# The last embedding's gate tiles 4 to 7 as seven Strassen block products, in a two-layer decoder step

## The chip, the cores and the metric

The kernel runs on one core of one Trainium2 chip. The metric is the device time of one execution in microseconds (us). In the profile the core's engines are PE (matrix multiply; PEld is its weight load), DVE (vector), ACT (scalar, with the activation functions), POOL (GpSimd) and SP (which issues the DMAs). Every computing engine takes its instructions in the order in which they stand in its queue.

## The reference

The kernel computes one inference step of a two-layer decoder for 512 prompt tokens and 32 sample tokens, in float32. Each layer ends with a gated embedding, and the change touches the second layer's, the last work of the kernel:

```python
D_MODEL, PLE_DIM = 1024, 256
def rmsnorm(x, g):
    xf = x.astype(jnp.float32)
    y = xf * lax.rsqrt(jnp.mean(xf * xf, axis=-1, keepdims=True) + EPS)
    return (y * g.astype(jnp.float32)).astype(x.dtype)
...
            h = h + 0.5 * swiglu(rmsnorm(h, ffn2_norm[i]), ffn2_w1[i], ffn2_w3[i], ffn2_w2[i])
            gate = jax.nn.sigmoid(rmsnorm(h, ple_norm[i]) @ ple_w_gate[i])
            h = h + gate * (pe[i] @ ple_w_proj[i])
```

## The kernel before, in words

The residual stream `h` lies transposed in SBUF, as eight chunks of 128 features by 544 tokens (T = 544, half of it HT = 272). Every float32 product is made of three float32r matmuls: weight and input are each split into a rounded part `hi` and a rest `lo`, and hi·hi, hi·lo and lo·hi are added in PSUM (`mm`, L286, L290, L292). A weight tile's split is an ACT cast and a DVE subtraction of 128x1024 (`_split`, L242 and L243); an input's is the same on 128x544 (`split_pair`, L330 and L331). One matmul takes 272 columns, so that an output tile of 128 features takes 8 x 3 x 2 = 48 matmuls.

The feed-forward layers already use a Strassen form with seven products in place of eight (`seven`, `forms`, `products`). Four weight blocks of 128x1024 give seven weight pieces, for four of which DVE makes a sum first (`_sum`, L228). The input side needs sums too: `forms` takes two chunks of `h`, scales both on ACT (L352), makes two combined tiles on DVE (one subtraction of 544 columns, L356, and two of 272, L358 and L359), and splits each into hi and lo (L330 on ACT, L331 on DVE). One product is 24 matmuls.

The last feed-forward layer ends with eight output tiles of its second matrix. After each, `update` adds it to the chunk `h[c]` on DVE (L578), and `on_chunk` (in `next_norm`) prepares the next norm: ACT scales by the gain (L342), DVE makes the rest (L343), ACT squares (L369) and POOL adds the square to `acc` (L371). The order on PE, DVE, ACT and POOL inside the feed-forward layer is the order of the code (`manual_schedule`); in the embedding the framework's scheduler orders each queue.

`ple` then makes the gates: eight tiles of 48 matmuls over the eight chunks in order. Beside the first or second of them `rstd` sums the squares over the partitions with four small matmuls (L408) and ACT and DVE make the reciprocal root (L386 to L393). Until that is done the gate tiles stay in PSUM; then DVE multiplies a tile by `rstd` (L766) and ACT takes the sigmoid (L767). A product with the embedding's own input follows two tiles behind (12 matmuls), is multiplied into the gate (L777), added to `h` (L778) and stored. There are three PSUM accumulators of the large kind (`ps`), used in turn, and two small ones (`pb`). Tile 7 is made in two column halves (`ple_last`), so that only a half's gate, product, sum and store follow the last matmul.

Weights are taken in the order of the list `pieces`; `prepare` loads, sums and splits them a few places ahead (`ahead`, 2 or 3 for splits and sums). Where the changed kernel is spoken of, its line numbers stand beside its own names: `ssq` and `update` have moved to L408, L410 and L617, the gate's multiplication and sigmoid to L782 and L783, product and addition to L793 and L794.

Of the kernel before, what the change touches and what calls it, by code (L numbers as in the profile page):

```python
# [23 lines left out]
F32R = mybir.dt.float32r  # L24
# [5 lines left out]
P = 128  # L30
# [108 lines left out]
class Builder:  # L139
# [588 lines left out]
    def ple_last(self, h, gates, rstd, xs, wp, pp, y):  # L728

        nc, tt = self.nc, self.nc.vector.tensor_tensor  # L730
        c = NC_ - 1
        a = self.tmp()
        outs = [self.pb(), self.pb()]
        self.cols_mm(outs, self.blocks(self.unit()), xs)
        for (u, v), out in zip(COLS, outs):
            tt(halves(a[:, u:v]), unwoven(out[:, :v - u]), halves(rstd[:, u:v]), ALU.mult)
            nc.scalar.activation(a[:, u:v], a[:, u:v], AF.Sigmoid)
        outs = [self.ps()[:, 0, :], self.ps()[:, 0, :]]
        self.cols_mm(outs, wp[2 * c:2 * c + 2], pp)
        for (u, v), out in zip(COLS, outs):  # L740
            tt(halves(a[:, u:v]), unwoven(out[:, :v - u]), halves(a[:, u:v]), ALU.mult)
            tt(h[c][:, u:v], h[c][:, u:v], a[:, u:v], ALU.add)
            nc.sync.dma_start(out=y[c][:, u:v], in_=h[c][:, u:v])

    def ple(self, h, box, layer, on_chunk):
        nc = self.nc
        xs = self.pairs(box)
        pp = []
        for c in range(2):
            raw = self.tmp()  # L750
            nc.sync.dma_start(out=raw, in_=self.i["pe"][layer, c])
            pair = self.big(F32R)
            self.split_pair(pair, raw)
            pp.append((pair[:, 0, :], pair[:, 1, :]))
        rstd, gates, wp = None, [], []
        last = layer == 1
        for c in range(NC_ + 2):
# [15 lines left out]
            for n in (range(c - 2, c + 1) if last and c == NC_ - 2 else [c - 2] if c >= 2 else ()):  # L773
# [597 lines left out]
    def build(self):  # L1371
# [7 lines left out]
        def ple_units(n):  # L1379
            for c in range(NC_):  # L1380
# [15 lines left out]
        ple_units(1)  # L1396

# [123 lines left out]
def _arrays(x_prompt, x_sample, p_prompt, p_sample, cache_k, cache_v, cache_logf, page_table, ffn1_norm, ffn1_w1,  # L1521
# [19 lines left out]
    a["wg"] = np.stack([_stationary(w) for w in ple_w_gate])  # L1541
    a["wp"] = np.stack([_stationary(w).reshape(2, 4, P, 2 * P).transpose(0, 2, 1, 3).reshape(2, P, 8 * P)
# [55 lines left out]
```

## Time and profile before

| What | Value |
|---|---|
| Time, median of 3 runs (lowest, highest) | 1933.02 us (1932.5, 1934.03) |
| The profiled execution's own time | 1931.65 us |
| Its span in the trace | 1929.9 us |
| PE busy | 1905.2 us, 99% of the span, 16508 matmuls |
| DVE busy | 1478.6 us, 77% |
| ACT busy | 949.0 us, 49% |
| POOL busy | 143.4 us, 7% |
| HBM read | 218.65 MB, written 16.44 MB: 122 GB/s over the span |

The profiled execution lies 1.37 us under the median, and its own time is 1.75 us above its span. A busy share says how long an engine had an instruction in it; for PE, whose matmuls overlap, the distance from one start to the next tells more. Times inside the span are counted from its start.

### The profile page before, as it was taken

What the parts mean: (1) busy time and instruction counts of PE and PEld (TensorE: products, weight loads), DVE (VectorE), ACT (ScalarE), POOL (GpSimd) and SP (SyncE); (2) the same over time, 40 slices, a digit from 0 to 9 for tenths busy, and PEclk for the clock granted to TensorE, in tenths of its full rate; (3) what the DMA queues carried; (4) which work ended last, traced back from release to release, by engine and by line L of the source; (5) the groups of instructions that cost most, each with busy time, mean ns of one, the idle gap of its engine ahead of it and who ended that gap; (6) DMA issues with size and microseconds to landing.
All of it is one profiled execution on the core that took longest, in us unless ns stands there. A gap on an engine that the chain in (4) does not pass through costs nothing.

```text
span 1929.9 us, 38975 instructions
## 1 busy us (share of the span) xinstructions
PE 1905.2 (99%) x16508; PEld 1869.9 (97%) x16508; DVE 1478.6 (77%) x1863; ACT 949.0 (49%) x1428; POOL 143.4 (7%) x190
## 2 busy tenths in 40 slices
PE   9999999999999999999999999999999999999999
PEld 8999999999999999999999999999977899999999
DVE  7878888556788888866578888887476888788874
ACT  7545444424555344454466444444374754444561
POOL 0000000400100000023000000002131300000020
PEclk9999999999999999999999999999999999999999
DMA  5233234312223232531484332323769332323431
GB/s 196 78 120 110 89 120 157 97 48 88 88 99 119 79 111 89 162 112 39 150 306 141 121 110 99 121 83 126 229 211 328 101 110 78 121 94 105 133 109 47
DMA packets 95743, 237.61 MB, mean 123 GB/s; under 512 B 11874, under 2 KB 29570, under 8 KB 95570
## 3 DMA queue, kind: packets, MB, share of 16 engines
q1 hardware_dynamic: 95426, 235.08, 36.6%
q8 instruction: 130, 2.13, 0.4%
q14 instruction: 43, 0.35, 0.1%
q10 hardware_dynamic: 144, 0.04, 0.0%
HBM read 218.65 MB, written 16.44 MB: 122 GB/s over the span
## 4 chain that ended last, share of the span: by engine, by line
PE 88%; DVE 6%; ACT 3%; issue 2%; DMA 1%; SPq 1%; POOL 0%; DVEq 0%; ACTq 0%; POOLq 0%
PE ps L539 31%; PE ps L286 15%; PE ps L292 15%; PE ps L290 15%; PE pb L539 5%; DVE big L243 2%; ACT big L242 1%; DVE big L228 1%; PE ps L892 1%; PE ps L893 1%; PE ps L894 1%; DVE big L331 1%; DVE big L497 0%; DMA tmp<-rows 0%; PE ps L1286 0%
## 5 line engine op out<-in xcount | busy, mean ns | idle before, releaser
L539 PE MATMUL ps<-big,big 128*128 128x272 f32 x5616 | 674.1, 279 | 5.9 <-DVE big L556 3.5
L539 PEld LDWEIGHTS ps<-big,big 128*128 128x128 f32 x5616 | 660.8, 189 | 7.0 <-issue 4.0
L243 DVE TENSOR_TENSOR big<-big,big 128x1024 fp32r<-128x1024 f32 (+2 forms) x537 | 587.1, 1096 | 91.0 <-ACT big L242 89.3
L242 ACT CAST big<-big 128x1024 fp32r<-128x1024 f32 (+2 forms) x537 | 484.2, 928 | 270.2 <-DVE big L228 267.7
L286 PE MATMUL ps<-big,big 128*128 128x272 f32 x2668 | 530.2, 280 | 2.9 <-ACT big L242 2.5
L292 PE MATMUL ps<-big,big 128*128 128x272 f32 x2668 | 528.3, 279 | 2.5 <-DVE big L243 2.3
L290 PE MATMUL ps<-big,big 128*128 128x272 f32 x2668 | 527.3, 279 | 0.3 <-DVE big L343 0.3
L286 PEld LDWEIGHTS ps<-big,big 128*128 128x128 f32 x2668 | 407.1, 189 | 7.8 <-ACT big L242 4.4
L292 PEld LDWEIGHTS ps<-big,big 128*128 128x128 f32 x2668 | 406.9, 189 | 4.5 <-DVE big L243 4.1
L290 PEld LDWEIGHTS ps<-big,big 128*128 128x128 f32 x2668 | 406.9, 189 | 0.7 <-DVE big L343 0.7
L371 POOL TENSOR_TENSOR st<-st,tmp 128x544 f32<-128x544 f32 (+1 forms) x63 | 87.4, 1387 | 1477.0 <-ACT tmp L369 1476.7
L228 DVE TENSOR_TENSOR big<-big,big 128x1024 f32<-128x1024 f32 x156 | 190.1, 1219 | 0.0
L578 DVE SCALAR_TENSOR_TENSOR big<-ps,big 128x544 f32<-128x544 f32 x160 | 115.3, 721 | 75.8 <-PE ps L292 75.8
L500 ACT ACTIVATE big<-big 128x544 f32<-128x544 f32 x88 | 57.9, 659 | 145.8 <-DVE big L497 144.6
L497 DVE TENSOR_TENSOR big<-big,st 128x1088 f32<-128x1088 f32 x88 | 113.6, 1293 | 3.9 <-ACT big L561 2.0
L547 ACT COPY tmp<-ps 128x544 f32<-128x544 f32 x117 | 71.5, 611 | 89.7 <-PE ps L539 89.7
L539 PE MATMUL pb<-big,big 128*128 128x272 f32 x936 | 114.8, 279 | 0.0
L539 PEld LDWEIGHTS pb<-big,big 128*128 128x128 f32 x936 | 111.3, 189 | 0.0
L342 ACT ACTIVATE big<-big,gains 128x544 fp32r<-128x544 f32 (+1 forms) x80 | 55.5, 702 | 91.3 <-DVE big L578 55.2
L331 DVE TENSOR_TENSOR big<-big,big 128x544 fp32r<-128x544 f32 (+1 forms) x112 | 79.2, 713 | 21.7 <-ACT big L330 21.5
L343 DVE SCALAR_TENSOR_TENSOR big<-big,gains,big 128x544 fp32r<-128x544 f32 (+1 forms) x80 | 64.6, 816 | 24.2 <-ACT big L342 24.2
L330 ACT CAST big<-big 128x544 fp32r<-128x544 f32 (+1 forms) x112 | 71.2, 643 | 18.9 <-DVE big L503 14.9
(218 smaller groups left out, 1388.5 us busy)
## 6 DMA issues: line engine op xcount, KB each, us to landing
big<-in_w SPq DMA_DIRECT2D x156, 512.0 KB
big<-in_w2a SPq DMA_DIRECT2D x64, 512.0 KB
big<-in_w2b SPq DMA_DIRECT2D x32, 384.0 KB
big<-in_w13p SPq DMA_DIRECT2D x16, 512.0 KB
big<-in_win SPq DMA_DIRECT2D x16, 512.0 KB
big<-in_wg SPq DMA_DIRECT2D x16, 512.0 KB
big<-in_ck SPq DMA_DIRECT2D x16, 512.0 KB
big<-in_cv SPq DMA_DIRECT2D x16, 512.0 KB
```

The lines of the kernel that those rows point to most:

```text
L228: self.nc.vector.tensor_tensor(t, a, b, ALU.add if op == "+" else ALU.subtract)
L242: self.nc.scalar.copy(hi, src)
L243: self.nc.vector.tensor_tensor(lo, src, hi.bitcast(F32), ALU.subtract)
L286: i = nc.tensor.matmul(o, wh, xh[:, b], start=s, stop=False)
L290: nc.tensor.matmul(o, wh, xl[:, b], start=False, stop=False)
L292: nc.tensor.matmul(o, wl, xh[:, b], start=False, stop=e)
L331: self.nc.vector.tensor_tensor(pair[:, 1, cols], src, pair[:, 0, cols].bitcast(F32), ALU.subtract)
L371: nc.gpsimd.tensor_tensor(acc[:, cols], acc[:, cols], sq, ALU.add)
L497: tt(g, g, rstd.unsqueeze(1).broadcast_to([P, 2, T]), ALU.mult)
L539: nc.tensor.matmul(turns(dst[w]), a[:, c], woven(b), start=k in "152" and kp == 0 and n == 0, stop=kp == NKP - 1 and n == 2, skip_group_ch ...
L547: nc.scalar.copy(t["r" + k], t["C" if k == "5" else "A"])
L578: nc.vector.scalar_tensor_tensor(halves(h[c]), whole(out), 0.5, halves(h[c]), ALU.mult, ALU.add)
```

## The change

In the second layer `ple` is replaced by a rewritten `ple_last`. Gate tiles 0 to 3 are made as before, with all four ahead of any product. Tiles 4 to 7 become one Strassen group (`strassen`): seven products of 24 matmuls into three accumulators, A and C of the large kind and B in the two small ones, with weight blocks from a new input `wg7`. The four sets of input forms that this needs are made in two places: pairs (0, 1) and (2, 3) while the feed-forward layer ends, behind its chunks 2 and 4 (`early={2: 0, 4: 1}`), pairs (4, 5) and (6, 7) beside gate tiles 2 and 3. The products with the embedding follow: 0 to 3 before the Strassen group, then 4, 6, 5, and 7 in two column halves. Only the product, not the gate, of tile 7 is halved now. In the diff `ple_input` is the loading that stood in `ple`.

```diff
+    def strassen(self, xf, done):
...
+        def step(k):
+            hi, lo = self.unit()
+            self.advance()
+            if k == "2":
+                t["B"] = [self.pb()[:, :HT] for _ in range(2)]
+            elif k in "15":
+                t["A" if k == "1" else "C"] = self.ps()[:, :, :HT]
+            out = t["A" if k in "1674" else "C" if k in "53" else "B"]
+            for kp in range(NKP):
+                xh, xl = xf[kp][k]
+                for n, (a, b) in enumerate(((hi, xh), (hi, xl), (lo, xh))):
+                    for w in range(2):
+                        c = slice(512 * w + P * kp, 512 * w + P * kp + P)
+                        nc.tensor.matmul(turns(out[w] if k == "2" else out[:, w]), a[:, c], woven(b),
...
+            if k in "156":
+                t["r" + k] = self.tmp().rearrange("p (w b) -> p w b", w=2)
+                nc.scalar.copy(t["r" + k], out)
+            elif k == "2":
+                t["g"] = self.big(), self.big()
+                for w in range(2):
+                    tt(halves(t["g"][0][:, w, :HT]), unwoven(out[w]), unwoven(t["r1"][:, w]), ALU.add)
+            elif k == "7":
+                tt(h4(t["g"][1][:, :, HT:]), u4(out), u4(t["r5"]), ALU.add)
+            elif k == "3":
+                tt(h4(t["g"][0][:, :, HT:]), u4(out), u4(t["r6"]), ALU.add)
+                done(0, t["g"][0])
+            else:
+                nc.scalar.copy(h4(t["g"][1][:, :, :HT]), u4(out))
+                done(1, t["g"][1])
+        return step
...
+    def ple_last(self, h, box, on_chunk):
+
+        nc, tt, y = self.nc, self.nc.vector.tensor_tensor, self.o["y"]
+        xs, xf, a, wp, rstd = self.pairs(box), box["f"], {}, [], None
+        pp = self.ple_input(1)
+        for c in range(4):
+            if c == 2:
+                self.ahead = (2, 3, 6)
+            if rstd is None:
+                p, rstd = self.tile_rstd(xs, box["acc"])
+            else:
+                p = self.tile_mm(xs)
+
+            def gate(c=c, p=p):
+                a[c] = self.tmp()
+                tt(halves(a[c]), whole(p), halves(rstd), ALU.mult)
+                nc.scalar.activation(a[c], a[c], AF.Sigmoid)
+            self.evac(gate)
+            if c >= 2:
+                xf.append(self.forms(h, G_PLE + 8, c, xs))
+            if c < 2:
+                wp += self.blocks(self.unit())
+
+        def product(n):
+            p = self.ps()
+            self.mm(p, wp[2 * n:2 * n + 2], pp, True, True)
+            tt(halves(a[n]), whole(p), halves(a[n]), ALU.mult)
+            tt(h[n], h[n], a[n], ALU.add)
+            on_chunk(n)
+
+        def done(k, g):
+            tt(g, g, rstd.unsqueeze(1).broadcast_to([P, 2, T]), ALU.mult)
+            nc.scalar.activation(g, g, AF.Sigmoid)
+            for w in range(2):
+                a[4 + 2 * w + k] = g[:, w]
+        for n in range(4):
+            product(n)
+        step = self.strassen(xf, done)
+        for k in SEVEN:
+            step(k)
+        for n in (4, 6, 5):
+            product(n)
         c = NC_ - 1
...
+            for c in range(4 if n else NC_):
                 self.add_plain(i["wg"][n, c])
...
         ple_units(1)
+        d = self.seven([i["wg7"][x] for x in range(4)])
+        self.pieces.extend(d[k] for k in SEVEN)
...
-        on, nxt = self.next_norm(h, G_PLE + 8)
+        on, nxt = self.next_norm(h, G_PLE + 8, early={2: 0, 4: 1})
         self.ffn(h, box, G_FFN2 + 8, None, on)
         box = nxt
-        self.ple(h, box, 1, lambda c: nc.sync.dma_start(out=o["y"][c], in_=h[c]))
+        self.ple_last(h, box, lambda c: nc.sync.dma_start(out=o["y"][c], in_=h[c]))
...
+    a["wg7"] = _pairs(ple_w_gate[1][:, D // 2:])
```

How the queues move, in three places. On DVE at the feed-forward layer's end (big_93 is the tile of chunks 2 and 3, big_94 of 4 and 5, big_95 of 6 and 7), before:

```order
L343 SCALAR_TENSOR_TENSOR big_22758<-big_93,gains,big_22758 128x544
L578 SCALAR_TENSOR_TENSOR big_93<-ps_22714,big_93 128x544
L243 TENSOR_TENSOR big_22803<-big_22592,big_22802 128x768
L343 SCALAR_TENSOR_TENSOR big_22808<-big_93,gains,big_22808 128x544
L578 SCALAR_TENSOR_TENSOR big_94<-ps_22764,big_94 128x544
```

and with the change:

```order
L343 SCALAR_TENSOR_TENSOR big_22758<-big_93,gains,big_22758 128x544
L356 TENSOR_TENSOR tmp_22767<-big_22764 128x544
L331 TENSOR_TENSOR big_22769<-tmp_22767,big_22769 128x544
L358 TENSOR_TENSOR tmp_22768<-big_22764,tmp_22767 128x272
L359 TENSOR_TENSOR tmp_22768<-big_22764,tmp_22768 128x272
L331 TENSOR_TENSOR big_22770<-tmp_22768,big_22770 128x544
L617 SCALAR_TENSOR_TENSOR big_93<-ps_22714,big_93 128x544
L243 TENSOR_TENSOR big_22817<-big_22592,big_22816 128x768
L343 SCALAR_TENSOR_TENSOR big_22822<-big_93,gains,big_22822 128x544
L617 SCALAR_TENSOR_TENSOR big_94<-ps_22778,big_94 128x544
```

Five instructions of the forms stand ahead of chunk 3's update; the same five stand ahead of chunk 5's, two updates on.

On DVE where `rstd` is finished and the gate tiles leave PSUM (ps_22982 before, ps_23010 now, is gate tile 0), before:

```order
L392 SCALAR_TENSOR_TENSOR tmp_23036<-pb_23030,tmp_23036 128x272
L243 TENSOR_TENSOR big_23193<-big_23116,big_23192 128x1024
L393 SCALAR_TENSOR_TENSOR st_23035<-tmp_23036,st_23035 128x544
L243 TENSOR_TENSOR big_23267<-big_23122,big_23266 128x1024
L766 TENSOR_TENSOR tmp_23057<-ps_22982,st_23035 128x544
L766 TENSOR_TENSOR tmp_23109<-ps_23060,st_23035 128x544
```

and with the change:

```order
L431 SCALAR_TENSOR_TENSOR tmp_23064<-pb_23058,tmp_23064 128x272
L432 SCALAR_TENSOR_TENSOR st_23063<-tmp_23064,st_23063 128x544
L228 TENSOR_TENSOR big_23152<-big_23144,big_23146 128x1024
L782 TENSOR_TENSOR tmp_23085<-ps_23010,st_23063 128x544
L782 TENSOR_TENSOR tmp_23137<-ps_23088,st_23063 128x544
L782 TENSOR_TENSOR tmp_23203<-ps_23154,st_23063 128x544
```

A weight sum (L228) stands between `rstd` and the first gate, as a split did before.

On DVE at the end, with the change (big_23484 holds the gates of tiles 4 and 6, big_23485 those of 5 and 7):

```order
L397 TENSOR_TENSOR big_23484<-ps_23395,tmp_23452 128x2x272
L798 TENSOR_TENSOR big_23484<-big_23484,st_23063 128x1088
L793 TENSOR_TENSOR big_23484<-ps_23571,big_23484 128x544
L798 TENSOR_TENSOR big_23485<-big_23485,st_23063 128x1088
L794 TENSOR_TENSOR big_94<-big_94,big_23484 128x544
L793 TENSOR_TENSOR big_23484<-ps_23587,big_23484 128x544
L793 TENSOR_TENSOR big_23485<-ps_23603,big_23485 128x544
L813 TENSOR_TENSOR big_23485<-ps_23619,big_23485 128x272
L794 TENSOR_TENSOR big_95<-big_95,big_23484 128x544
L794 TENSOR_TENSOR big_94<-big_94,big_23485 128x544
L813 TENSOR_TENSOR big_23485<-ps_23620,big_23485 128x272
L814 TENSOR_TENSOR big_95<-big_95,big_23485 128x272 x2
```

Before, the queue ended with one half tile's four instructions of 272 columns (L741, L742, L741, L742) behind tile 7's last product; now two multiplications of 1088 columns, three products and three additions of 544 stand there too.

## Rows read from the trace of the kernel before

**Rows 1.** The profile's page, section 1: busy us (share of the span) xinstructions.

```profile
PE 1905.2 (99%) x16508; PEld 1869.9 (97%) x16508; DVE 1478.6 (77%) x1863; ACT 949.0 (49%) x1428; POOL 143.4 (7%) x190
```

**Rows 2.** Busy time of each engine in four stretches at the end, with granted clock.

```profile
core 0: us, PE busy (x) PEld busy (x) DVE busy (x) ACT busy (x) POOL busy (x), PEclk, DMA share, GB/s
1849.00:1870.00 21.00, 21.00 (x184) 21.00 (x183) 14.21 (x18) 12.03 (x17) 9.65 (x6) 1.00 0.34 106
1870.00:1884.00 14.00, 14.00 (x123) 14.00 (x122) 12.50 (x15) 11.79 (x15) 1.34 (x1) 1.00 0.01 2
1884.00:1919.00 35.00, 35.00 (x305) 35.00 (x304) 15.09 (x21) 5.77 (x8) 0.00 (x0) 1.00 0.10 37
1919.00:1926.10 7.10, 6.98 (x61) 6.78 (x59) 3.16 (x7) 0.86 (x2) 0.00 (x0) 1.00 0.27 101
```

**Rows 3.** Timeline of PE, the last 60 matmuls: start us, us, line, xcount.

```profile
1918.87 5.72 PE L723 MATMUL pb<-big,big 128*128 128x272 f32 x48
1924.43 1.55 PE L723 MATMUL ps<-big,big 128*128 128x272 f32 x12
```

**Rows 4.** Timeline of DVE, the feed-forward layer's end: start us, us, [idle before].

```profile
1852.84 0.77 DVE L343 SCALAR_TENSOR_TENSOR big<-big,gains,big 128x544 fp32r<-128x544 f32 x1
1853.54 0.71 DVE L578 SCALAR_TENSOR_TENSOR big<-ps,big 128x544 f32<-128x544 f32 x1
...
1861.62 0.72 DVE L578 SCALAR_TENSOR_TENSOR big<-ps,big 128x544 f32<-128x544 f32 x1 [1.62 <-PE ps L292]
...
1869.96 0.72 DVE L578 SCALAR_TENSOR_TENSOR big<-ps,big 128x544 f32<-128x544 f32 x1 [1.62 <-PE ps L292]
1871.50 0.79 DVE L343 SCALAR_TENSOR_TENSOR big<-big,gains,big 128x544 fp32r<-128x544 f32 x1 [0.82 <-ACT big L342]
1872.58 2.14 DVE L331 TENSOR_TENSOR big<-tmp,big 128x544 fp32r<-128x544 f32 x2 [0.30 <-ACT big L330]
```

**Rows 5.** Groups of instructions by line and shape: xcount | busy us, mean ns.

```profile
L356 DVE TENSOR_TENSOR tmp<-big 128x544 f32<-128x544 f32 x16 | 11.9, 744 | 5.3 <-ACT big L352 5.1
L358 DVE TENSOR_TENSOR tmp<-big,tmp 128x272 f32<-128x272 f32 x16 | 7.6, 476 | 0.5
L331 DVE TENSOR_TENSOR big<-tmp,big 128x544 fp32r<-128x544 f32 x44 | 32.9, 756 | 5.8 <-ACT big L330 5.2
L352 ACT ACTIVATE big<-big,gains 128x544 f32<-128x544 f32 x32 | 22.1, 740 | 0.0
L330 ACT CAST big<-tmp 128x544 fp32r<-128x544 f32 x44 | 28.1, 645 | 41.4 <-DVE tmp L695 17.9 <-DVE tmp L356 13.9 <-DVE tmp L359 9.4
L243 DVE TENSOR_TENSOR big<-big,big 128x1024 fp32r<-128x1024 f32 x377 | 464.7, 1236 | 77.3 <-ACT big L242 76.9
L228 DVE TENSOR_TENSOR big<-big,big 128x1024 f32<-128x1024 f32 x156 | 190.1, 1219 | 0.0
L497 DVE TENSOR_TENSOR big<-big,st 128x1088 f32<-128x1088 f32 x88 | 113.6, 1293 | 3.9 <-ACT big L561 2.0
L767 ACT ACTIVATE tmp<-tmp 128x544 f32<-128x544 f32 x15 | 9.6, 655 | 39.9 <-DVE tmp L766 39.9
```

**Rows 6.** Timeline of POOL, two of its seven additions at the feed-forward layer's end.

```profile
1853.00 1.82 POOL L371 TENSOR_TENSOR st<-st,tmp 128x544 f32<-128x544 f32 x1 [0.90 <-ACT tmp L369]
...
1872.15 1.34 POOL L371 TENSOR_TENSOR st<-st,tmp 128x544 f32<-128x544 f32 x1 [2.61 <-ACT tmp L369]
```

**Rows 7.** Timeline of DVE: the first two gates, and the last four instructions.

```profile
1884.62 1.35 DVE L766 TENSOR_TENSOR tmp<-ps,st 128x544 f32<-128x544 f32 x2
...
1926.23 0.43 DVE L741 TENSOR_TENSOR tmp<-ps,tmp 128x272 f32<-128x272 f32 x1
1926.70 0.44 DVE L742 TENSOR_TENSOR big<-big,tmp 128x272 f32<-128x272 f32 x1
```

**Rows 8.** Timeline of PE, a wait in an earlier feed-forward layer.

```profile
546.58 1.63 PE L539 MATMUL ps<-big,big 128*128 128x272 f32 x12 [2.14 <-DVE big L556]
```

**Rows 9.** Busy time of each engine in the stretch around that wait, with granted clock.

```profile
540.00:552.00 12.00, 9.86 (x86) 9.69 (x85) 12.00 (x16) 7.29 (x10) 0.00 (x0) 1.00 0.12 34
```

More of the change, by code (lines that the diff above doesn't have):

```diff
@@ L364, in forms @@
                 "5": half(f13, 0), "7": half(f13, 1), "6": half(f24, 0), "4": half(f24, 1)}
+    def strassen(self, xf, done):
+        nc, tt, t = self.nc, self.nc.vector.tensor_tensor, {}
+        u4 = lambda t: t.rearrange("p w (b a) -> p w a b", a=2)
+        h4 = lambda t: t.rearrange("p w (a b) -> p w a b", a=2)
+        def step(k):
[12 more added lines that the diff above has]
+                        nc.tensor.matmul(turns(out[w] if k == "2" else out[:, w]), a[:, c], woven(b),
+                                         start=k in "152" and kp == 0 and n == 0, stop=kp == NKP - 1 and n == 2,
+                                         skip_group_check=True)
+            if k in "156":
[14 more added lines that the diff above has]
+        return step
     def ssq(self, acc, h, cols=slice(0, T), first=False):
@@ L740, in ple_last, with ple_input @@
         for (u, v), out in zip(COLS, outs):
-            tt(halves(a[:, u:v]), unwoven(out[:, :v - u]), halves(a[:, u:v]), ALU.mult)
-            tt(h[c][:, u:v], h[c][:, u:v], a[:, u:v], ALU.add)
+            tt(halves(a[c][:, u:v]), unwoven(out[:, :v - u]), halves(a[c][:, u:v]), ALU.mult)
+            tt(h[c][:, u:v], h[c][:, u:v], a[c][:, u:v], ALU.add)
             nc.sync.dma_start(out=y[c][:, u:v], in_=h[c][:, u:v])
+    def ple_input(self, layer):
+        pp = []
+        for c in range(2):
+            raw = self.tmp()
+            self.nc.sync.dma_start(out=raw, in_=self.i["pe"][layer, c])
+            pair = self.big(F32R)
+            self.split_pair(pair, raw)
+            pp.append((pair[:, 0, :], pair[:, 1, :]))
+        return pp
     def ple(self, h, box, layer, on_chunk):
@@ L747, in ple @@
         xs = self.pairs(box)
[L748 to L754, printed above, removed]
+        pp = self.ple_input(layer)
         rstd, gates, wp = None, [], []
-        last = layer == 1
         for c in range(NC_ + 2):
@@ L772, in ple @@
                 wp += [(hi[:, P * k:P * k + P], lo[:, P * k:P * k + P]) for k in range(8)]
-            for n in (range(c - 2, c + 1) if last and c == NC_ - 2 else [c - 2] if c >= 2 else ()):
+            for n in [c - 2] if c >= 2 else ():
                 p2 = self.ps()
@@ L779, in ple @@
                 on_chunk(n)
-            if last and c == NC_ - 2:
-                self.ple_last(h, gates, rstd, xs, wp, pp, self.o["y"])
-                return
     def square(self, raw):
@@ L1379, in ple_units @@
         def ple_units(n):
-            for c in range(NC_):
+            for c in range(4 if n else NC_):
                 self.add_plain(i["wg"][n, c])
```

11 lines of the change are left out of this document (3 added, 8 removed).

## The prediction

> **What bounds the kernel now.** I read the busy shares first. PE is busy 99% of the span and every other engine far less [rows 1]. Then the stretches of the part that changes: PE is busy in all of 1849 to 1919 and in 6.98 of the last 7.10 us, at a granted clock of 1.00, its higher level of 2.4 GHz [rows 2]. The reader is to see that nothing waits here for anything but PE, so removed matmuls pay in full, and every wait that the change brings PE is paid in full too. PE's timeline gives the price of a matmul: 48 take from 1918.87 to 1924.43, which is 0.1158 us each [rows 3]. Last, I read what DVE, ACT and POOL do in the feed-forward layer's last 20 us, where two sets of forms are put in. DVE is busy 14.21 of 21 us there and 12.50 of the next 14 [rows 2]. That is where the room is least.
>
> **What it removes.** Four gate tiles of 48 matmuls (192) become seven products of 24 (168). 24 x 0.1158 = **2.78 us** less on PE. Everything else on PE stays in number. This is also the most that the change can win.
>
> **What it puts in at the feed-forward layer's end.** I carried the new order forward by hand, instruction by instruction, with durations of rows: 0.72 for a DVE operation of 544 columns [rows 4], 0.44 for 272 [rows 7], 0.65 for a cast and 0.74 for a scaling on ACT, 1.22 for a weight's subtraction or sum [rows 5]. A DVE instruction starts some 0.08 before the one ahead of it ends (1853.54 against 1852.84 + 0.77 [rows 4]).
>
> POOL's additions matter here. The two subtractions that start at 1872.58 take 2.14 together, where two of the mean 0.756 would take 1.43; POOL adds from 1872.15 to 1873.49 [rows 4 to 6]. The other way round, the addition at 1853.00 takes 1.82 and not 1.34, behind the DVE instruction that runs to 1853.61 [rows 4, 6]. So I let each wait for the other where both read SBUF twice. The Trainium skill's page "SBUF — State Buffer", section "SBUF: two separate sides", has this as a rule: DVE with two SBUF inputs and GpSimd share one port pair, an exclusive lock, and the later one blocks fully; what the sum would be by the group means alone, without such waits, is +0.1 us in place of +2.4. These two rows side with waiting.
>
> First set (pair 0, 1): the scalings end on ACT at 1854.1. Then DVE and ACT take turns: 0.72, cast 0.65, 0.72, 0.44, 0.44, cast 0.65, 0.72, which is 4.34, some 0.1 for handoffs and 0.65 of waiting for POOL. DVE is free at 1859.1, and chunk 3's update comes then instead of at 1853.54 [rows 4]. PE does not notice: it needs that accumulator for chunk 6 only at 1861.4. Chunk 4's update comes at 1861.4.
>
> Second set (pair 2, 3): chunk 4's rest waits for POOL and ends at 1865.9, the forms take 4.4 again, and chunk 5's update runs from 1870.1 to 1870.9 instead of starting at 1861.62 [rows 4]. The accumulators go round by threes, so gate tile 0 takes chunk 5's. PE reaches it at 1869.8 (the last update of before starts at 1869.96, just behind PE's last matmul [rows 4]) and **waits 1.1**. Chunk 6's update follows at 1872.6 and chunk 7's at 1875.7, with a weight's subtraction and a rest before each; before, chunk 7's was at 1869.96. Tile 0 takes the chunks in order. It needs chunk 6's rest 38 matmuls in, at 1875.3, and has it at 1875.8 (**0.5**); chunk 7's rounded part at 1876.3, and has it at 1877.2 (**0.9**); then its rest at 1878.0 (**0.6**). Together 3.2 us.
>
> **The norm's root and the first gates.** The last square is added at 1879.4, its sum split at 1881.3; the four small matmuls stand 34 matmuls into gate tile 1, no longer 13, and end at 1883.5. ACT is done at 1885.0 and DVE at 1888.75, a weight's subtraction between; then the sum L228 (1.22) stands ahead of the first gate. That starts at 1889.8, not at 1884.62 [rows 7], and frees its accumulator at 1890.5. Gate tile 3 wants it at 1890.1: **0.5** more.
>
> **The seven products.** Each is 2.78 us of PE. On DVE four pieces cost 2.44 (sum and split), three 1.22, and the remaining forms, gates and sums lie between. By the same carrying forward the tightest piece, that of product "3", is ready 0.8 before PE wants it. I cost this at nothing; what hides it is the products before it, and past those 0.8 each us is paid.
>
> **The end.** Before, PE's last matmul ends at 1925.98 [rows 3] and DVE at 1927.14 [rows 7], 1.16 later. Now both 1088-column multiplications (1.29 each [rows 5]) and their sigmoids follow the last two products. Behind product "4" DVE does, without a pause, a product 0.72, the multiplication 1.29, five operations of 0.72 and four of 0.44: 7.4 less ten overlaps of 0.08, so 6.6. PE has 37 matmuls left, 4.3. DVE ends 2.5 after PE, **1.3 worse**, and tile 7's second half waits 0.2 for an accumulator. A sigmoid of 1088 columns stands in no row: not under 0.655, not over 1.31 [rows 5]; I take 1.10, a slope as between shapes of one operation, and the upper end costs 0.3.
>
> **Sum.** -2.8 + 3.2 + 0.5 + 0.2 + 1.3 = **+2.4 us**. On the profiled execution (span 1929.9, own time 1931.65) that is 1934.0. The median of the runs lies 1.37 higher, at 1933.02, so I forecast **1935.4**. A measurement of this kernel can tell about 0.2%, 3.9 us, from no change: this is within it.
>
> The bounds: without POOL's waits +0.1; with nothing waiting but the tail -1.5; with POOL's waits at their largest +4.8 (below).
>
> **Rivals.**
>
> *The slack takes it.* The turns between ACT and DVE go faster than I carried them, or the additions miss the forms. Tile 0 then waits for little. With no wait of PE at all the time would be 1933.0 - 2.8 + 1.3 = 1931.5. For it: before, DVE stands idle 1.62 ahead of chunks 5 and 7's updates [rows 4], so there is room in the stretch. Against: five instructions and two casts that follow each other take 4.3 whatever the room, and two such sets stand between chunks 2 and 5.
>
> *The additions fall wholly into the forms.* This one ends slower. Four additions lie in the second set's stretch. I gave them some 0.5 to 0.7 of waiting each; if each holds a DVE instruction for its whole 1.34 [rows 6], that is 0.6 more four times: +2.4 on chunk 7's update, and so on gate tile 0. The time is 1937.8. It decides from an update of chunk 7 later than about 1877.2: that is 1.5 beyond my 1875.7, where the loss passes 3.9. For it: the pair at 1872.58 lost 0.7 to one addition. Against: DVE waits mostly for a remainder.
>
> *PE's clock falls.* The waits at tile 0 come in pieces, 3.2 us in some 9. A wait of 2.14 in an earlier layer [rows 8] leaves the granted clock of its stretch at 1.00 [rows 9]. At 1.2 GHz a matmul of 272 columns would take 0.1158 more; one gate tile of 48, 5.6 us: 1941. The Trainium skill's page "TensorE: Matmul & The Clock Gate", section "What's actually happening", says that the array's clock is throttled by default and that activity releases it; no row here shows a fall inside the work.
>
> That the change does not do what it says can be left out: the order shows 168 matmuls and the forms at their places.
>
> **How the numbers follow.** Forecast (POOL's waits as carried, +1 to +3.9): 0.61. Slack: 0.24. Additions wholly in the forms: 0.12. Clock: 0.02. The rest, 0.01, is a scatter of the measurement by which even the full 2.8 would count as faster. Faster by over 0.2% needs 3.9 us and PE can give 2.8, so 0.02 with that scatter; slower takes the third and fourth rival, 0.14; 0.84 is within. The range reaches from the slack's 1931.5 to just short of the third rival's time, 1937.6.
>
> **What would show it.** In the new profile: 24 matmuls fewer; chunk 7's update (L617) 5 to 6 us after PE's last matmul of that tile has ended; waits of PE of about 1 us at gate tile 0's start and near its end, released by DVE L617, ACT L342 and DVE L343; the first gate (L782) more than 10 us behind chunk 7's update and a wait of some 0.5 at gate tile 3; no wait inside the seven products; and DVE ending about 2.5 us after PE. I am wrong if PE runs through gate tile 0 without a wait, if it waits for weight pieces inside the products, or if the clock there is under 1.00.

## The result and the profile after

| | us, median (lowest to highest, runs) |
|---|---|
| the change | 1936.22 (1933.88 to 1937.66, 16) |
| before, beside it | 1932.63 (1931.36 to 1934.03, 16) |
| ratio | 1.0017, 95% interval 1.0011 to 1.0024 |

The change is slower by 0.17%, by that ratio some 3.3 us (the medians lie 3.6 apart): a loss that shows, within the 0.2% that counts as no change. The forecast was 1935.4 (+2.4). The profiled execution of the change took 1934.78 us with a span of 1933.0, 3.1 above that of before.

The page, section 1, after (busy us, share of the span, instructions), against [rows 1]:

```profile
PE 1904.0 (99%) x16484; PEld 1867.5 (97%) x16484; DVE 1501.3 (78%) x1891; ACT 963.4 (50%) x1448; POOL 142.8 (7%) x190
```

24 matmuls fewer, as said, and 28 instructions more on DVE, 20 more on ACT. Where PE stands still shows in its timeline around gate tile 0 (start us, us, line, xcount, idle time before and what ended it) and at the last matmuls:

```profile
1870.61 0.47 PE L286 MATMUL ps<-big,big 128*128 128x272 f32 x2 [0.70 <-DVE big L617]
...
1876.41 0.50 PE L290 MATMUL ps<-big,big 128*128 128x272 f32 x2 [1.16 <-DVE big L343]
...
1877.83 0.50 PE L286 MATMUL ps<-big,big 128*128 128x272 f32 x2 [0.68 <-ACT big L342]
1878.65 0.50 PE L290 MATMUL ps<-big,big 128*128 128x272 f32 x2 [0.32 <-DVE big L343]
...
1890.57 0.40 PE L292 MATMUL ps<-big,big 128*128 128x272 f32 x2
1891.09 0.47 PE L286 MATMUL ps<-big,big 128*128 128x272 f32 x2
...
1925.91 1.85 PE L762 MATMUL ps<-big,big 128*128 128x272 f32 x12
```

L617 is now the update of a chunk, L342 and L343 are its rounding and rest. What a wait costs is the distance from one matmul's start to the next, less the 0.1158 of an unhindered one: 0.86, 1.33, 0.85 and 0.48 us here, and the matmul behind each restart comes late once more, by 0.07 to 0.10. Together 3.89. The same measure gives 0.36 at gate tile 3 (1891.09 above) and 0.29 at tile 7's second half; inside the seven products it gives nothing. PE ends at 1927.76. That is the sum of its parts: 1925.98 [rows 3] - 2.78 + 3.89 + 0.36 + 0.29 = 1927.74.

Why the waits come, in DVE's timeline, with [rows 4] beside it:

```profile
1854.16 1.23 DVE L356 TENSOR_TENSOR tmp<-big 128x544 f32<-128x544 f32 x1 [0.56 <-ACT big L352]
1856.10 0.72 DVE L331 TENSOR_TENSOR big<-tmp,big 128x544 fp32r<-128x544 f32 x1 [0.71 <-ACT big L330]
...
1858.37 0.73 DVE L331 TENSOR_TENSOR big<-tmp,big 128x544 fp32r<-128x544 f32 x1 [0.71 <-ACT big L330]
1859.01 0.72 DVE L617 SCALAR_TENSOR_TENSOR big<-ps,big 128x544 f32<-128x544 f32 x1
...
1869.75 0.72 DVE L617 SCALAR_TENSOR_TENSOR big<-ps,big 128x544 f32<-128x544 f32 x1
...
1871.51 0.78 DVE L343 SCALAR_TENSOR_TENSOR big<-big,gains,big 128x544 fp32r<-128x544 f32 x1
1872.21 0.72 DVE L617 SCALAR_TENSOR_TENSOR big<-ps,big 128x544 f32<-128x544 f32 x1
1872.84 1.74 DVE L243 TENSOR_TENSOR big<-big,big 128x1024 fp32r<-128x1024 f32 x1
1874.51 1.85 DVE L343 SCALAR_TENSOR_TENSOR big<-big,gains,big 128x544 fp32r<-128x544 f32 x1
1876.28 0.71 DVE L617 SCALAR_TENSOR_TENSOR big<-ps,big 128x544 f32<-128x544 f32 x1
```

The first set is done at 1859.1. Behind the second, chunk 5's update comes at 1869.75, which [rows 4] have at 1861.62, and chunk 7's at 1876.28, not at 1869.96. Chunk 5's and chunk 6's rests are the same operation, yet one takes 0.78 and the other 1.85. POOL's timeline shows what else runs then: it adds from 1874.40 on, 0.11 before the slow rest starts (no_additions, below, tests this).

```profile
1871.94 1.56 POOL L410 TENSOR_TENSOR st<-st,tmp 128x544 f32<-128x544 f32 x1 [7.08 <-ACT tmp L408]
1874.40 1.37 POOL L410 TENSOR_TENSOR st<-st,tmp 128x544 f32<-128x544 f32 x1 [0.90 <-ACT tmp L408]
```

The end, on DVE, against the last two of [rows 7] (L798 multiplies a pair of tiles by the root, L793 and L813 the gates by the embedding's products, L794 and L814 are the sums):

```profile
1921.08 1.29 DVE L798 TENSOR_TENSOR big<-big,st 128x1088 f32<-128x1088 f32 x1
1923.55 0.73 DVE L793 TENSOR_TENSOR big<-ps,big 128x544 f32<-128x544 f32 x1 [1.18 <-ACT big L799]
1924.19 1.28 DVE L798 TENSOR_TENSOR big<-big,st 128x1088 f32<-128x1088 f32 x1
1925.38 0.72 DVE L794 TENSOR_TENSOR big<-big,big 128x544 f32<-128x544 f32 x1
1926.02 1.35 DVE L793 TENSOR_TENSOR big<-ps,big 128x544 f32<-128x544 f32 x2
...
1929.25 0.79 DVE L814 TENSOR_TENSOR big<-big,big 128x272 f32<-128x272 f32 x2
```

The 1.18 us that DVE waits at 1923.55 are for ACT's sigmoid of 1088 columns (L799):

```profile
1922.40 1.11 ACT L799 ACTIVATE big<-big 128x1088 f32<-128x1088 f32 x1 [6.65 <-DVE big L798]
```

DVE ends at 1930.04, 2.28 after PE, where it was 1.16.

### The profile page after: what moved, and what is told of

Its sections match the earlier page's. It is cut to its first block, busy times and chain, and to the rows that moved or that the text cites. A ratio compares the mean times of both kernels' runs of the same rounds, so it can differ in the third digit from the quotient of the medians.

```text
span 1933.0 us, 38973 instructions
## 1 busy us (share of the span) xinstructions
PE 1904.0 (99%) x16484; PEld 1867.5 (97%) x16484; DVE 1501.3 (78%) x1891; ACT 963.4 (50%) x1448; POOL 142.8 (7%) x190
## 3 DMA queue, kind: packets, MB, share of 16 engines
q8 instruction: 130, 2.13, 0.4%
## 4 chain that ended last, share of the span: by engine, by line
PE 87%; DVE 7%; ACT 3%; issue 1%; DMA 1%; SPq 0%; POOL 0%; DVEq 0%; ACTq 0%; POOLq 0%
PE ps L578 31%; PE ps L286 14%; PE ps L292 14%; PE ps L290 14%; PE pb L578 5%; DVE big L243 2%; ACT big L242 1%; DVE big L228 1%; PE ps L964 1%; PE ps L965 1%; PE ps L966 1%; PE ps L384 1%; DVE big L536 0%; DVE big L331 0%; PE ps L1358 0%
## 5 line engine op out<-in xcount | busy, mean ns | idle before, releaser
L578 PE MATMUL ps<-big,big 128*128 128x272 f32 x5616 | 674.1, 279 | 5.9 <-DVE big L595 3.5
L578 PEld LDWEIGHTS ps<-big,big 128*128 128x128 f32 x5616 | 660.8, 189 | 7.0 <-issue 4.0
L286 PE MATMUL ps<-big,big 128*128 128x272 f32 x2620 | 520.6, 280 | 4.8 <-ACT big L242 2.8
L292 PE MATMUL ps<-big,big 128*128 128x272 f32 x2620 | 518.9, 279 | 2.4 <-DVE big L243 2.2
L290 PE MATMUL ps<-big,big 128*128 128x272 f32 x2620 | 518.5, 279 | 1.8 <-DVE big L343 1.8
L286 PEld LDWEIGHTS ps<-big,big 128*128 128x128 f32 x2620 | 399.7, 189 | 10.2 <-ACT big L242 5.6
L292 PEld LDWEIGHTS ps<-big,big 128*128 128x128 f32 x2620 | 399.7, 189 | 4.5 <-DVE big L243 4.0
L290 PEld LDWEIGHTS ps<-big,big 128*128 128x128 f32 x2620 | 399.5, 189 | 2.7 <-DVE big L343 2.6
L228 DVE TENSOR_TENSOR big<-big,big 128x1024 f32<-128x1024 f32 x160 | 195.1, 1220 | 0.0
L617 DVE SCALAR_TENSOR_TENSOR big<-ps,big 128x544 f32<-128x544 f32 x160 | 115.3, 721 | 69.9 <-PE ps L292 69.9
L342 ACT ACTIVATE big<-big,gains 128x544 fp32r<-128x544 f32 (+1 forms) x80 | 55.4, 702 | 86.5 <-DVE big L617 50.2
L343 DVE SCALAR_TENSOR_TENSOR big<-big,gains,big 128x544 fp32r<-128x544 f32 (+1 forms) x80 | 66.9, 844 | 24.2 <-ACT big L342 24.1
```

The costliest lines, as they stand in the source:

```text
L228: self.nc.vector.tensor_tensor(t, a, b, ALU.add if op == "+" else ALU.subtract)
L286: i = nc.tensor.matmul(o, wh, xh[:, b], start=s, stop=False)
L290: nc.tensor.matmul(o, wh, xl[:, b], start=False, stop=False)
L292: nc.tensor.matmul(o, wl, xh[:, b], start=False, stop=e)
L578: nc.tensor.matmul(turns(dst[w]), a[:, c], woven(b), start=k in "152" and kp == 0 and n == 0, stop=kp == NKP - 1 and n == 2, skip_group_ch ...
L617: nc.vector.scalar_tensor_tensor(halves(h[c]), whole(out), 0.5, halves(h[c]), ALU.mult, ALU.add)
```

## The experiments

All are edits of the changed kernel. Up to the part that changes, the same instructions end up to 6.7 us earlier or later from one profiled execution to the next (the stretch below starts between 1852.04 and 1858.76), so spans can't be compared. Falls of PE's clock are part of this (last section). The last 600 matmuls are the same in all (in before, the last 624), so each trace is read from the start of the first of these (1853.54 in before and in the change) to PE's end, and to the end of the execution. "Waits" is the sum of distances above 0.1158, as above.

| kernel | to PE's end | to the end | waits | median us | ratio to before (95%) |
|---|---|---|---|---|---|
| before | 72.44 | 76.34 | 0 | | |
| the change | 74.22 | 79.42 | 4.5 | 1936.22 | 1.0017 (1.0011 to 1.0024) |
| after_again | 74.22 | 79.41 | 4.5 | 1936.50 | 1.0022 (1.0013 to 1.0031) |
| two_sets_out | 69.84 | 75.03 | 0.2 | 1931.99 | 1.0000 (0.9991 to 1.0009) |
| second_set_out | 69.89 | 75.07 | 0.2 | 1930.67 | 0.9994 (0.9985 to 1.0003) |
| one_set_early | 74.27 | 79.48 | 4.6 | 1936.48 | 1.0023 (1.0014 to 1.0033) |
| chunk_earlier | 73.74 | 78.93 | 4.1 | 1934.95 | 1.0018 (1.0008 to 1.0027) |
| no_additions | 71.02 | 76.20 | 1.3 | 1933.28 | 1.0006 (0.9997 to 1.0015) |
| in_steps_1_4 | 71.43 | 76.61 | 1.8 | 1932.73 | 1.0004 (0.9995 to 1.0013) |
| in_steps_no_additions | 69.90 | 75.08 | 0.2 | 1931.34 | 0.9997 (0.9988 to 1.0007) |
| last_sums_on_pool | 73.93 | 80.02 | 4.3 | 1936.52 | 1.0023 (1.0012 to 1.0033) |
| last_sums_out | 75.03 | 79.21 | 5.4 | 1934.72 | 1.0018 (1.0008 to 1.0028) |
| in_steps_two_sums | 70.17 | 75.26 | 0.5 | 1931.05 | 0.9996 (0.9987 to 1.0005) |
| in_steps_two_sums_again | 70.16 | 75.22 | 0.5 | 1931.60 | 0.9997 (0.9988 to 1.0006) |

after_again repeats the change beside others:

> The changed kernel itself once more, on the same chip and beside the same runs of before as the two others. Ratio to before 1.0011 to 1.0024 again; from the 600th last matmul to the end of the execution 79.4 us again, with waits of TensorE of 4.5 us in sum.

It came out so; the traces of the two agree within 0.01 us, so differences of some tenths in the second and third columns can be trusted.

### Is it the two sets? two_sets_out

```
+        xf[:0] = list(xf)
...
-        on, nxt = self.next_norm(h, G_PLE + 8, early={2: 0, 4: 1})
+        on, nxt = self.next_norm(h, G_PLE + 8)
```

> Leaves out the two sets of forms that are made in the feed-forward layer's last chunks (pairs 0 and 1, 2 and 3); the seven products use the two later sets twice. Nothing else moves. Theory (the loss is VectorE's delay by these two sets in the last chunks): TensorE's four waits at the start of gate tile 0 (0.86, 1.33, 0.85 and 0.48 us in the changed kernel's trace, 3.5 in sum) fall below 0.3 in sum, chunk 7's update starts before 1873.5 instead of 1876.28, and the time falls by 3 to 4 us against the changed kernel, to 1932.2 to 1933.2. Rival (the group of seven products and the tail lose the time, by evictions and sums that end 2.28 us after the last matmul): the waits at gate tile 0 may go, but others of like size come later in the gate stage, and the time stays within 1.5 us of the changed kernel's 1936.2.

The waits at gate tile 0 and 3 are gone. DVE stands idle ahead of chunk 7's update as it did before [rows 4]:

```profile
1875.18 0.72 DVE L617 SCALAR_TENSOR_TENSOR big<-ps,big 128x544 f32<-128x544 f32 x1 [1.62 <-PE ps L292]
```

This trace runs 5.22 later than the change's (1858.76 against 1853.54), so that is 1869.96 there, as before the change: the rival falls. PE's part is 69.84 = 72.44 - 2.78 + 0.17, so the removed matmuls pay in full and the sets cost all of 4.4 us. To the end it is still only 1.31 below before, since the tail stays longer.

### Which of the two? second_set_out and one_set_early

second_set_out makes the first set as the change does, and none after chunk 4:

```
+        xf.insert(1, xf[0])
...
-        on, nxt = self.next_norm(h, G_PLE + 8, early={2: 0, 4: 1})
+        on, nxt = self.next_norm(h, G_PLE + 8, early={2: 0})
```

> Of the two sets in the feed-forward layer's last chunks the first (after chunk 2) stays and the second (after chunk 4) is left out; the seven products use the first set twice, the other two sets stay beside gate tiles 2 and 3. Theory (VectorE can work off one set before chunk 6, the waits all come of the second): no wait of over 0.2 us at gate tile 0; from the 600th last matmul to the last one 69.8 us, as without both sets, where the changed kernel has 74.2, and the end about 4.3 us earlier; a time like that of the kernel without both sets, 1931.5 to 1932.5. Rival (each set costs about half): 2 to 2.5 us of waits stay, from the 600th last matmul to the last 72 us, time 1933.5 to 1934.5.

The first set alone, with the additions, costs nothing (75.07 against 75.03): the stretch has room for it. The waits come only when the second stands behind it; the second without the first was not run. one_set_early makes that one, too, but beside the gate tiles:

```
-            if c >= 2:
+            if c >= 1:
...
-        on, nxt = self.next_norm(h, G_PLE + 8, early={2: 0, 4: 1})
+        on, nxt = self.next_norm(h, G_PLE + 8, early={2: 0})
```

> Of the two sets of forms that the change puts into the feed-forward layer's last chunks only the first stays there (after chunk 2); the other three are made beside gate tiles 1 to 3. Theory (chunks 3 to 5 had slack for one set, the second set after chunk 4 is what makes chunk 6 and 7 late): the first set's delay is worked off before chunk 6, TensorE's waits at gate tile 0 fall from 3.5 us to under 0.6, and the time is 2.5 to 3.5 us below the changed kernel, 1932.7 to 1933.7. Rival (any set in the chunks makes the last chunks late, since ScalarE and VectorE hand work to and fro there): half of the waits stays, 1.5 to 2 us, time 1934.2 to 1935. Second rival (VectorE cannot make three sets beside the gate tiles): waits of over 1 us appear at gate tile 2 or 3 or at the first product, and the time is 1935 or more.

Half of this failed. Tile 0 runs through, and the loss comes back whole, later on PE:

```profile
1891.47 0.50 PE L286 MATMUL ps<-big,big 128*128 128x272 f32 x2 [2.54 <-ACT big L242]
1903.51 5.33 PE L384 MATMUL ps<-big,big 128*128 128x272 f32 x44 [0.65 <-DVE tmp L793]
```

At gate tile 3 it is not that DVE is full: in this run it is busy for 17.30 of the 22 us from 1872 to 1894. What is late is the cast of that tile's weight on ACT. It stands in ACT's queue behind the first gates' sigmoids and the set's casts, and ACT waits 3.25 us for the first gate:

```profile
1886.89 1.28 ACT L783 ACT_TABLE_LOAD   x1 [3.25 <-DVE tmp L782]
...
1890.38 1.99 ACT L242 CAST big<-big 128x1024 fp32r<-128x1024 f32 x2
```

In the change the same cast, the seventh of the stretch, stands well ahead of the gates (at 1882.30). From 1891.45 on DVE has no pause, and the second wait is at the first of the seven products, for an accumulator that DVE frees late.

### A chunk earlier: chunk_earlier

```
-        on, nxt = self.next_norm(h, G_PLE + 8, early={2: 0, 4: 1})
+        on, nxt = self.next_norm(h, G_PLE + 8, early={1: 0, 3: 1})
```

> Both sets of the feed-forward layer's last chunks are made one chunk earlier, whole, after chunks 1 and 3 instead of 2 and 4. Theory (VectorE has too little free time in these chunks for two whole sets, with its waits for ScalarE inside each set and GpSimd's additions; a set holds up all that stands behind it): the lateness of chunks 6 and 7 shrinks, but chunk 4 or 5's update now comes so late that TensorE waits about 2 us for the accumulator ahead of chunk 7's or gate tile 0's products; waits in sum 3.2 to 4.2 us, time within 1 us of the changed kernel. Rival (the second set only starts too late): waits at gate tile 0 fall to 1.5 us or less in sum with none before them, and the time falls by 2 to 3 us.

As the theory had it: 4.1 us of waits, the largest now ahead of chunk 7's product, which wants the accumulator of chunk 4.

```profile
1867.46 0.47 PE L286 MATMUL ps<-big,big 128*128 128x272 f32 x2 [1.94 <-DVE big L617]
```

### What makes a set so long: no_additions, in_steps_1_4, in_steps_no_additions

no_additions leaves POOL's additions of squares out:

```
-        if not first:
+        if not first and add:
             nc.gpsimd.tensor_tensor(acc[:, cols], acc[:, cols], sq, ALU.add)
```

> Leaves out the seven additions that GpSimd makes of the squares for this norm (the sum of squares holds chunk 0's alone); all forms stay as in the changed kernel. Theory (VectorE's operations on two SBUF operands are held up while GpSimd adds): the rounding step of chunk 6's rest falls from 1.85 us to 0.8, the difference of a form from 1.74 to 1.2, and one of 2.15 to about 1.45; TensorE's waits at gate tile 0 fall by 1.5 to 2.3 us and the time by as much, to 1934 to 1934.7. Rival (the waits come of the number of operations on VectorE, and the lengthened ones lie in time that it would have waited anyhow): the rows get shorter but the waits shrink by under 0.5 us, time 1935.7 or more.

More came back than the theory said: 3.2 us. The two operations of chunk 6 that took 1.74 and 1.85 in the change:

```profile
1875.19 1.21 DVE L243 TENSOR_TENSOR big<-big,big 128x1024 fp32r<-128x1024 f32 x1
1876.33 0.78 DVE L343 SCALAR_TENSOR_TENSOR big<-big,gains,big 128x544 fp32r<-128x544 f32 x1
```

This agrees with the Trainium skill's page "SBUF — State Buffer", section "SBUF: two separate sides", by which DVE with two SBUF inputs and GpSimd shut each other out for a whole instruction.

in_steps_1_4 keeps the additions, and makes each set in four pieces, three of them ahead of the rests of the chunks that follow (the first set starts a chunk earlier):

```
+    def form_steps(self, h, gcol, n, xs, out):
...
+        yield
+        nc.vector.tensor_tensor(two(t13), x[:, :, HT:], two(x[:, 0, :]), ALU.subtract)
+        nc.vector.tensor_tensor(t24[:, :HT], x[:, 1, HT:], t13[:, :HT], ALU.subtract)
+        nc.scalar.copy(f13[:, 0, :], t13)
+        yield
...
+            for s in list(running):
+                if next(s, 0) == 0:
+                    running.remove(s)
+            self.nc.vector.scalar_tensor_tensor(
...
-        on, nxt = self.next_norm(h, G_PLE + 8, early={2: 0, 4: 1})
+        on, nxt = self.next_norm(h, G_PLE + 8, early={1: 0, 4: 1}, steps=True)
```

> The same two sets in steps: after chunk 1 and chunk 4 only their scaled copies are made, and at each of the three chunks that follow one piece of VectorE's and ScalarE's work on a set, ahead of that chunk's own rounding, so that neither engine stands waiting for the other inside a set. Theory (part of what the sets cost is VectorE's idle time inside a set: 0.56, 0.71 and 0.71 us of waiting for ScalarE per set in the trace of the kernel with one set early): waits at gate tile 0 fall from 3.5 us to about 2.2 and the one at gate tile 3 goes; the time falls by 1.2 to 1.8 us. Rival (the work itself is too much, or ScalarE's extra copies now hold up VectorE's differences for the weights): waits stay at 3.5 us or grow.

2.8 us came back, more than expected, and the waits fell from 4.5 to 1.8. It is idle time that came back. From the stretch's start to the end of chunk 7's rest the windows (columns as in [rows 2]) have in the change and here:

```profile
1853.54:1878.60 25.06, 22.24 (x186) 21.46 (x184) 20.64 (x25) 14.76 (x22) 7.05 (x6) 1.00 0.27 87
1854.78:1877.34 22.56, 21.48 (x186) 21.28 (x184) 20.77 (x27) 15.28 (x23) 7.78 (x6) 1.00 0.31 96
```

DVE is busy as long as in the change, 20.77 against 20.64, and idle for 1.79 in place of 4.42, so its operations are held up by POOL about as much as there. A part of this may be the first set's earlier start; moving both sets whole by a chunk gave 0.5 back (chunk_earlier). What is left stands at chunk 7's rest (L679 here): PE's wait, then DVE's operation, then POOL's two additions together.

```profile
1877.39 0.50 PE L290 MATMUL ps<-big,big 128*128 128x272 f32 x2 [1.13 <-DVE big L679]
```
```profile
1875.74 1.60 DVE L679 SCALAR_TENSOR_TENSOR big<-big,gains,big 128x544 fp32r<-128x544 f32 x1 [0.19 <-ACT big L675]
```
```profile
1875.03 3.52 POOL L435 TENSOR_TENSOR st<-st,tmp 128x544 f32<-128x544 f32 x2 [3.50 <-ACT tmp L433]
```

in_steps_no_additions does both:

> Both sets in steps after chunks 1 and 4, as in the run before, and GpSimd's seven additions of squares for this norm left out (the sum of squares is chunk 0's alone). Theory (what the steps leave of the wait at gate tile 0, 1.30 us, is VectorE held up by GpSimd's additions: its rounding of chunk 7 takes 1.60 there instead of 0.78): no wait of over 0.2 us is left in gate tiles 0 to 3, and from the 600th last matmul to the end of the execution the kernel takes 75.0 to 75.3 us, as with the sets left out (75.03 and 75.07), where the one with additions takes 76.61, before 76.34 and the change 79.42. Rival (the sets' own work on VectorE is too much even so): 0.5 us or more of waits stay, 75.6 us or more.

75.08, as with the sets left out. So both sets' own work fits into the stretch. What does not fit is what surrounds it: 2.8 us come back by the order alone, 3.2 by the additions alone, 4.3 by both.

### The tail: last_sums_on_pool and last_sums_out

```
-            tt(h[n], h[n], a[n], ALU.add)
+            (nc.gpsimd.tensor_tensor if n >= 4 else tt)(h[n], h[n], a[n], ALU.add)
```

> The sums of output chunks 4, 6 and 5 (0.72 and two of 0.68 us on VectorE) are made on GpSimd; nothing else moves. Theory (the tail's 2.28 us after TensorE's last matmul, 1.16 before the change, is VectorE working off what the sigmoid of the second gate tile left late): VectorE's last operation comes about 1.1 us after the last matmul plus the two halves' own work, the end is 0.8 to 1.2 us earlier, time 1935.0 to 1935.4. Rival (GpSimd's sums take over 1.3 us each and hold up VectorE's last two sums, or end themselves after VectorE): the tail stays at 2 us or more and the time within 0.4 us of the changed kernel's 1936.2.

The rival was right: the end comes 0.6 later. DVE's last two sums, 0.79 in the change, take 1.93, and POOL needs 4.91 for three that DVE does in 2.1:

```profile
1929.02 1.93 DVE L814 TENSOR_TENSOR big<-big,big 128x272 f32<-128x272 f32 x2
```
```profile
1925.39 4.91 POOL L794 TENSOR_TENSOR big<-big,big 128x544 f32<-128x544 f32 x3 [44.54 <-DVE big L793]
```

last_sums_out makes none of the three:

```
+            if n < 4:
                 tt(h[n], h[n], a[n], ALU.add)
```

> Leaves out VectorE's sums of output chunks 4, 5 and 6 with the embedding products (0.72 and 2 x 0.68 us); these chunks are stored without them. Theory (after the seven products VectorE works without a pause until the end, so the tail is its queue): VectorE ends 1.2 to 1.5 us after TensorE's last matmul instead of 2.28, and the end comes 0.9 to 1.2 us earlier. Rival (the tail is the store of the last chunk, or the second gate tile's sigmoid): VectorE's end moves, the end of the span does not, or the waits for the sigmoid grow by what the sums gave back.

From PE's end to the end it is 4.18 where the change has 5.20: 1.02 earlier, as the theory said, though three sums take 2.1. The rest goes to the second sigmoid, for which DVE now waits:

```profile
1926.88 0.72 DVE L793 TENSOR_TENSOR big<-ps,big 128x544 f32<-128x544 f32 x1 [0.54 <-ACT big L800]
```

So the tail is DVE's queue and, right behind it, the sigmoid. The stretch as a whole is only 0.2 shorter, and the ratio to before did not fall (1.0018): PE's part is 0.8 longer in this trace, for a reason of its own (last section).

### Put together: in_steps_two_sums

Against in_steps_1_4 the first set's last piece moves to chunk 3 and the second's behind chunk 7's rest, and the sums of chunks 4 and 6 go to POOL:

```
+            (nc.gpsimd.tensor_tensor if n in (4, 6) else tt)(h[n], h[n], a[n], ALU.add)
...
+        on, nxt = self.next_norm(h, G_PLE + 8, steps={(1, 2): [0], (2, 0): [0], (3, 0): [0], (3, 2): [0], (4, 2): [1], (5, 0): [1], (6, 0): [1], (7, 1): [1]})
```

Here (4, 2) is chunk 4, behind its square; 0 is ahead of the chunk's rest, 1 behind it.

> The version that the runs so far point to: both sets in steps after chunks 1 and 4, the first set's last piece already at chunk 3 and the second's after chunk 7's rounding; the sums of output chunks 4 and 6 on GpSimd, that of 5 on VectorE. Theory: the wait at gate tile 0 shrinks by some 0.5 us more, the tail after TensorE's last matmul by 0.3 to 0.4; from the 600th last matmul to the end of the execution 75.4 to 76.0 us where before takes 76.34, so 0.3 to 0.9 us below before, a ratio of 0.9995 to 0.9998 that the timing can hardly tell from 1. Rival (the last piece now holds up the root of the norm and gate tile 3, or GpSimd's sums hold up tile 7's): 76.6 us or more.

> The version with both sets in steps and the sums of output chunks 4 and 6 on GpSimd once more, unchanged. In its first profile the stretch from the 600th last matmul to the end took 75.26 us where before takes 76.34, which is 0.0006 of the time; its first timing gave a ratio of 0.9996 with an interval of 0.9987 to 1.0005. Theory: 75.3 us again, and a ratio of 0.9992 to 0.9998. Rival (the profile was a lucky one): 76 us or more, a ratio of 1 or above.

Both profiles show the stretch 1.1 us shorter than in before, and 0.5 us of waits. Chunk 7's rest takes 1.22 now, not 1.60:

```profile
1874.25 1.22 DVE L684 SCALAR_TENSOR_TENSOR big<-big,gains,big 128x544 fp32r<-128x544 f32 x1 [0.82 <-ACT big L682]
```

The gain is PE's part. From PE's end to the end it is 5.09 and 5.06, against 5.20 in the change: the sums on POOL gave 0.1 there, not the 0.3 to 0.4 expected.

This version is faster than the change beside which it ran (1931.05 against 1936.50, with intervals of their ratios that do not touch). Against before, both intervals take in 1: the profiles say 0.0006 less, the timing does not tell it.

## Why the prediction was right

The likeliest case was the one that happened, with the mechanism, the places and the sign forecast: 1936.22 against 1935.4, inside the range. By its steps:

- **What it removes**, 2.78: shown. two_sets_out has just this on PE, but for 0.17 at tile 7.
- **The sets**, 3.2 of waits at gate tile 0 (the four waits given, 1.1, 0.5, 0.9 and 0.6, add up to 3.1): measured 3.89, at the four places named and with the releasers named. DVE's times held until chunk 6 (updates of 3 to 6 at 1859.01, 1861.24, 1869.75, 1872.21; said 1859.1, 1861.4, 1870.1, 1872.6). Then one term was too small: the wait for chunk 6's rest, 0.5 said, 1.33 measured. I had let that rest run its plain 0.78; an addition of POOL's fell onto nearly all of it (1.85). A second term was missing: the late matmul behind each of the four restarts, 0.37 in all. The other three waits were 0.86, 0.85 and 0.48, which is 0.41 less than said.
- **Gate tile 3**, 0.5: 0.36. **Tile 7**, 0.2: 0.29. **Seven products**, nothing: nothing.
- **The end**, 1.3 worse: 1.12 between PE's and DVE's ends, and the rest of the execution 0.18 longer. The working itself, 6.6 on DVE less 4.3 on PE, gives 2.3 and not the 2.5 written down; 2.28 was measured. The sigmoid of 1088 columns, which no row had, took 1.11 (1.10 taken).
- The sum was +2.4; the trace says +3.1, and the timing some 3.3. Chunk 6's rest (0.8) and the restarts (0.4) are the greater part of what the terms missed.

That the number came within 0.8 of the measured one is in part luck: it stood on 1933.02, the median of three runs of before, and the sixteen beside the change have 1932.63.

One sign was missed narrowly: chunk 7's update comes 6.4 us after PE's last matmul of its tile has ended (1869.92), not 5 to 6.

The rivals: "the slack takes it" held for one set and not for two (second_set_out). "The additions fall wholly into the forms" set its mark at chunk 7's update later than 1877.2; it came at 1876.28, between my 1875.7 and that mark. Of this rival a part happened: two additions fell for the most part on one operation each, but on the rests of chunks 4 (1.87, for which I had allowed) and 6 (1.85, for which I had not), while the second set's forms ran at 0.71, 0.73, 0.43, 0.44 and 0.73, unhindered. The additions cost 3.2 us of the 4.5 (no_additions), where I had weighed them at 2.3 (+2.4 with, +0.1 without). The clock's rival did not decide here. PE's granted clock at gate tile 0 is 1.00 in the change's trace (columns as in [rows 2]):

```profile
1870.00:1878.00 8.00, 5.54 (x43) 5.17 (x44) 7.18 (x8) 4.52 (x8) 2.93 (x2) 1.00 0.10 37
```

But what I held against it, that the wait of [rows 8] leaves the clock at 1.00, holds in nine of the 14 profiles; in the other five the same wait is followed by a fall (last section).

What the forecast did not see is that the order inside a set is as dear as the additions: I counted the turns between ACT and DVE as fixed, and in_steps_1_4 got 2.8 us back by giving DVE something else to do meanwhile (idle for 1.79 us in place of 4.42).

## What to carry to other kernels

When work is moved onto an engine that has free time, its own duration need not be what costs: ask what the in-order queue behind it waits for while it stands, and whether another engine works on the same memory at that moment. Where one piece fits, two may not, and a move to the next stage only moves the wait if some queue there holds up other work behind it, even on an engine that is not full. Where whole times scatter by more than the effect, compare the stretch from a common instruction on.

## What was not expected of the hardware

PE's granted clock falls inside the work, in some executions and not in others. All 14 profiles have the wait of 2.13 to 2.14 us of [rows 8]. In nine of them the clock from 548 to 552 is 1.00; in five (after_again, two_sets_out, one_set_early, no_additions, last_sums_on_pool) it is 0.57 to 0.75. In after_again, PE's timeline and the window behind the wait (columns as in [rows 2]):

```profile
546.99 9.20 PE L578 MATMUL ps<-big,big 128*128 128x272 f32 x63 [2.14 <-DVE big L595]
```
```profile
548.00:552.00 4.00, 4.00 (x27) 4.00 (x26) 4.00 (x6) 2.18 (x4) 0.00 (x0) 0.70 0.00 0
```

In last_sums_out it falls in the part that changes. The four waits at gate tile 0 are those of the change (0.69, 1.16, 0.69 and 0.32 us idle, against 0.70, 1.16, 0.68 and 0.32), and behind the last of them the clock is down. The windows of that kernel, with the same columns:

```profile
1872.00:1876.00 4.00, 2.84 (x25) 2.64 (x23) 4.00 (x4) 1.30 (x2) 2.01 (x2) 1.00 0.99 312
1876.00:1880.00 4.00, 2.99 (x15) 2.59 (x14) 2.89 (x4) 3.41 (x6) 1.34 (x1) 0.67 0.77 251
1880.00:1884.00 4.00, 4.00 (x33) 4.00 (x33) 4.00 (x5) 3.74 (x4) 0.00 (x0) 0.90 0.38 149
```

In its timeline two matmuls take 0.66 there, not 0.40, and start 0.227 apart, which is 1.2 GHz in place of 2.4:

```profile
1878.85 0.66 PE L286 MATMUL ps<-big,big 128*128 128x272 f32 x2
```

It made the distances there 1.5 us longer; 0.36 of this came back, since gate tile 3 then did not wait, so PE's part is 1.1 longer than in last_sums_on_pool, which has the same waits up to there. Of four profiles with these same waits (the change, after_again, last_sums_on_pool, last_sums_out) one shows it, so waits of PE can cost more than their length, in some executions. Whether this is why the timed loss (3.3 and 4.3 us) lies above the traces' 3.1 was not shown. The runs timed with after_again point to it: those with a mean granted clock of 1.000 average 1934.8 (two runs) against 1931.6 for before (twelve), 3.2 apart; the others average 1936.6 and 1932.4, 4.2 apart.

The Trainium skill's page "TensorE: Matmul & The Clock Gate", section "What's actually happening", has the clock throttled by default and released by activity; these falls, each behind waits of PE, agree with it.

A matmul behind a restart is late too: in the change's trace the second one starts 0.19 to 0.22 after the first, not 0.1158, behind each of the six waits.
